# A hybrid encoder trunk: the last convolution products between the first heads' turns and the first scores, and x's operands and first sums reordered

## The chip, the cores and the metric

The kernel runs on one core of one Trainium2 chip. Its engines are TensorE (PE in the profile, with PEld for its weight loads), VectorE (DVE), ScalarE (ACT), GpSimd (POOL) and SyncE (SP), which here only issues DMAs. Each engine takes its instructions from a queue of its own, in order; semaphores tie them together. The metric is the device time of one execution in microseconds; lower is better.

## The reference

Two layers act on x, 512 tokens by 1024 features, in float32. Each layer is

```python
x = x + 0.5 * swiglu(rms_norm(x, ffn1_norm[l]), ffn1_w_gate[l], ffn1_w_up[l], ffn1_w_down[l])
h = rms_norm(x, mix_norm[l])
p = h @ w_in[l]
attn = mla_group(p[..., :o_kv], p[..., o_kv:o_pe], p[..., o_pe:o_cv], ...)
conv = conv_group(p[..., o_cv:], conv_w[l], conv_b[l], conv_ln_g[l], conv_ln_b[l])
x = x + jnp.concatenate([attn, conv], axis=-1) @ w_out[l]
x = x + 0.5 * swiglu(rms_norm(x, ffn2_norm[l]), ffn2_w_gate[l], ffn2_w_up[l], ffn2_w_down[l])
x = rms_norm(x, post_norm[l])
```

`mla_group` makes queries and keys of 8 heads (96 features each) from low-rank latents, normalises them per head, and runs block-causal softmax attention. `conv_group` takes two halves a and g of 512 channels, forms a * sigmoid(g), convolves each channel with 31 taps along the tokens, and applies a layer norm and a silu. The inner width of `swiglu` is 2816.

## The kernel before

**Layout.** x lies transposed in on-chip memory: 8 tiles of 128 features by 512 tokens. Every product of float32 operands is made of three (`mm3`, L142 to L145): each operand is split into a rounded high part and a low rest, and high-high, high-low and low-high are summed in PSUM. One output tile of 128 by 512 over 1024 inputs is thus 8 x 3 = 24 products. Weights come through `load_w` (L126): a DMA on SP's queue into a raw tile (three buffers), a cast to the high part on ScalarE (L130), the low part on VectorE (L136); high and low tiles have four buffers each. For the first four tiles of w_out the low part comes from ScalarE (L133) and a DMA issued by GpSimd (L134).

**Order of the work.** The program is written as a Python trace. When the kernel is built, a scheduler fills each engine's queue by the order of the trace and by a simulated clock: what is traced earlier goes first where it is ready in that simulation. `tc.issue_after(ins)` adds that whatever the block traces on the engine of `ins` stands behind `ins` in that engine's queue. On the chip the queues are fixed. PSUM has 7 banks in one pool (`bank()`) and one more for the convolution on VectorE.

**FFN** (`ffn_body`). The inner width is worked through in four chunks (`CHUNKS`). In the first chunk four outputs are made by plain products (`plain`, `plain_out`): p = 0 with r = 0 and 1, then p = 1 with r = 0 and 1. x is not normalised ahead of them; the norm is a factor R per token, applied in `plain_out`. Calling `norm()` once makes the sums of squares over all features (eight narrow matmuls at L186), and from them 1/sqrt per token (VectorE, GpSimd); the second call spreads it over the partitions (a product at L205) and copies it to R. From R on, a generator `operands(R)` makes the normalised x and its sums and differences, in 31 steps, which the later chunks need for a Strassen-like product (`pair`, seven products instead of eight). `advance(n)` traces n of these steps: 6 after each output of p = 1, and 3 after each of the 8 down products of the first chunk. In the very first FFN the first weights (`w0`) are loaded beside x, and the squares of x are made by ScalarE and summed by VectorE (L179) at the start.

**Mix** (`mix_body`). `SEQ` (L40) gives the order of its steps: query latents (`q0`, `q1`, `q2`), convolution inputs of four channel groups (first one untitled, then `c1`, `c2`, `c3`), latent keys, `uq` (queries), `uk` (keys and values), and last `c2` and `c3`. A convolution input is two groups of 24 products (`conv_in`) and a gate `glu` (L429): VectorE scales the second group by R (L431), ScalarE takes the sigmoid (L433), VectorE scales the first group (L435) and multiplies (L437). Then the attention: for each head `turn` transposes q and k on TensorE into two banks (L616, L621) and has them evacuated by ScalarE (L618) and VectorE (L623); `scores` (L639) makes four blocks of scores in three banks, VectorE takes their maxima (L641) and ScalarE the exponentials (L645); `turn_p` (L660), `values` (L673) and `turn_out` (L691) follow with lags of some steps (`ORDER`), so that the heads overlap. Traced behind the attention, and so filling idle time, is the convolution (L704 to L723): groups 0 and 3 on VectorE (L712), groups 1 and 2 by products on ScalarE (L716) that GpSimd adds up (L720). The sum of the four (L734 to L736) is read by a product on TensorE (L738) for the layer norm's mean, and the output projection ends the mix.

In the queue of TensorE before the change, the first scores stand as follows: both groups of `c3`, the turns of heads 0 and 1, the scores of head 0, the turn of head 2, the scores of head 1, and so on.

Of the kernel before, what the change touches and what calls it, by code (L numbers as in the profile page):

```python
# [11 lines left out]
AF = mybir.ActivationFunctionType  # L12
# [23 lines left out]
RING = 41  # L36
CHUNKS = ((0, 2), (2, 5), (5, 8), (8, 11))
CONV = "DAAD"
PAUSE = 16
SEQ = "q0 R c1 q1 q2 qo k kt tt uq uk c2 c3"  # L40
POOLW = "wo"
QFOLD = 0
GLUP = 0
# [24 lines left out]
def encoder_kernel(ctx: ExitStack, tc: tile.TileContext, xT, consts, vecs, rgain, wgu1, wd1,  # L68
# [22 lines left out]
    def bank():  # L91
        return psum.tile([P, S], FP, tag="ps", name=nm("ps"))
# [148 lines left out]
    def ffn_body(fpool, l, gx, norm, wgu, wd, gain, done, w0):  # L241
# [12 lines left out]

        def plain(os, ws, ks):
            for gu, o in enumerate(os):
                for k in ks:
                    w = ws[k % 2]
                    c = slice(gu * 512 + k // 2 * P, gu * 512 + (k // 2 + 1) * P)
                    mm3(o, w[0][:, c], w[1][:, c], gx[k][0], gx[k][1], k == 0, k == KD - 1)  # L260
# [118 lines left out]
        for p0, p1 in CHUNKS:  # L379
            f0, fn = 2 * p0, 2 * (p1 - p0)  # L380
            act = []
            for p in range(p0, p1):
                if p == 0:
                    os = []
                    for r in range(2):
                        ws = w0 if r == 0 and w0 else [load_w(wgu[l, p, 2 * r + q], WC) for q in range(2)]
                        os.append([bank(), bank()])
                        plain(os[r], ws, range(KD - 1))
                        plain(os[r], ws, range(KD - 1, KD))
                        R = norm()  # L390
                    steps = operands(R)
                    for o in os:
                        act.append(plain_out(o, R))
                elif p < CHUNKS[0][1]:
                    for r in range(2):
                        ws = [load_w(wgu[l, p, 2 * r + q], WC) for q in range(2)]
                        o = [bank(), bank()]
                        plain(o, ws, range(KD))
                        advance(6)
                        act.append(plain_out(o, R))  # L400
                else:
                    act += pair(p)
            for m in range(KD):
                pd = bank()
                group(pd, load_w(wd[l, m, :, f0 * P:(f0 + fn) * P], fn * P), act, range(fn), fn)
                if p0 == 0:
                    advance(3)
                V.scalar_tensor_tensor(x[:, m, :], pd, 0.5, x[:, m, :], ALU.mult, ALU.add)  # L408
                if p1 == NF // 2:
                    done(m)  # L410
            if p0 == 0:
                advance(99)
# [12 lines left out]
    def mix_body(kpool, l, gx, norm, done):  # L425
# [3 lines left out]
        def glu(pa, pg):  # L429
            tg = tmp()  # L430
            V.tensor_tensor(tg, pg, R, ALU.mult)  # L431
            sg = tmp()
            A.activation(sg, tg, AF.Sigmoid)  # L433
            ta = tmp()
            V.tensor_tensor(ta, pa, R, ALU.mult)  # L435
            uc = slot()
            (G if GLUP else V).tensor_tensor(uc, ta, sg, ALU.mult)  # L437
            u.append(uc)
# [174 lines left out]
        def turn(h):  # L613
# [4 lines left out]
            A.activation(qT[0:DQ], ps[0:DQ], AF.Copy, scale=gqs[0:DQ])  # L618
            ps = bank()
            for t in range(NT):  # L620
                T.transpose(ps[0:DQ, t * P:(t + 1) * P], kn[:, t, h], ident)  # L621
            kT = slot()
            V.tensor_scalar(kT[0:DQ], ps[0:DQ], gk, None, ALU.mult)  # L623
            heads[h]["qk"] = qT, kT
# [67 lines left out]
            at.append(split(ps))  # L692

        STAGES = [({"t": turn, "s": scores, "p": turn_p, "v": values, "o": turn_out}[c], int(d)) for c, d in zip(ORDER[::2], ORDER[1::2])]
        for step in range(H + 6):
            for stage, lag in STAGES:
                if 0 <= step - lag < H:
                    stage(step - lag)


        with tc.issue_after(order["keys"]):
# [252 lines left out]
```

## Time and profile before

| what | value |
|---|---|
| time, median of 3 runs | 1857.87 us (1856.27 to 1859.78) |
| the profiled execution, its own time | 1857.87 us |
| its span, first to last instruction | 1856.1 us |
| mean granted clock of TensorE | 0.992 of full speed |
| ScalarE's busy time | 937.3 us (50%) |
| VectorE's busy time | 1354.5 us (73%) |
| GpSimd's busy time | 334.2 us (18%) |

The profile is of one execution. A row of the timeline gives the start in us from the span's beginning, the duration, the engine, the line of the kernel, the operation, the tile written, the tiles read, the sizes, how many alike were merged, and in brackets the idle time of the engine just before, with the instruction that ended it. Durations of neighbouring matmuls overlap, since they are pipelined: their spacing is the difference of the starts. A view of windows gives for each stretch its length, the busy time and count of PE, PEld, DVE, ACT and POOL, the clock granted to TensorE, the DMA engines' share and GB/s. In the view of waits a row is: engine, tile and line that waited, whom for, us in total, times, the longest.

### The profile page before, as it was taken

The page shows a single profiled execution, that of the slowest core. Times are in us where ns is not written, and L with a number is a line of the kernel's source. Part 1 is how long each engine was busy: PE and PEld are TensorE (multiplying, and loading weights), DVE is VectorE, ACT ScalarE, POOL GpSimd, SP SyncE. Part 2 cuts the span into 40 slices and gives each one's busy share as a digit, 9 for nine tenths or more (in the row PEclk, how much of TensorE's full clock was granted, in tenths as well). Part 3 has the DMA queues.
Part 4 walks back from the last instruction along what each step waited for, and adds up shares of the span by engine and source line. Part 5 has one row for each costly group of instructions (what it writes and reads, how often), then busy time and mean ns, then how long its engine had stood idle before and what let it go on. Part 6 is the DMA issues. An engine that isn't in the chain of part 4 may idle for free.

```text
span 1856.1 us, 27852 instructions
## 1 busy us (share of the span) xinstructions
PE 1815.4 (98%) x11248; PEld 1623.2 (87%) x11248; DVE 1354.5 (73%) x1764; ACT 937.3 (50%) x1470; POOL 334.2 (18%) x238
## 2 busy tenths in 40 slices
PE   8999999999999999999999999999999999999997
PEld 6898989888788798989888999998978788989895
DVE  6885767588956985757779676766978659767673
ACT  4453535457943453535635444444778434535352
POOL 1000000248933000000310000002688410000002
PEclk9999999999999999999999999999999999999998
DMA  5142422324123142422512424223250322424221
GB/s 218 52 148 68 137 63 86 114 78 133 35 75 102 29 151 66 139 67 94 169 52 72 140 66 140 66 83 114 72 148 1 118 70 63 143 62 143 63 86 63
DMA packets 55569, 175.72 MB, mean 95 GB/s; under 512 B 6160, under 2 KB 6544, under 8 KB 55440
## 3 DMA queue, kind: packets, MB, share of 16 engines
q1 hardware_dynamic: 53856, 169.37, 29.2%
q0 software_dynamic: 1152, 4.19, 1.3%
q8 instruction: 88, 1.44, 0.3%
q10 hardware_dynamic: 432, 0.38, 0.1%
q14 instruction: 41, 0.34, 0.1%
HBM read 171.82 MB, written 2.10 MB: 94 GB/s over the span
## 4 chain that ended last, share of the span: by engine, by line
PE 81%; DVE 9%; ACT 4%; POOL 3%; issue 2%; DMA 0%; SPq 0%; DVEq 0%; POOLq 0%; ACTq 0%
PE ps L143 25%; PE ps L145 25%; PE ps L144 25%; PE ps L673 2%; PE ps L639 2%; DVE wl L136 2%; ACT pr L716 1%; DVE r L292 1%; POOL y L720 1%; PE ps L660 1%; DVE t L297 1%; DVE cv L712 1%; DVE x L408 1%; ACT wh L130 1%; POOL sck L161 0%
## 5 line engine op out<-in xcount | busy, mean ns | idle before, releaser
L143 PE MATMUL ps<-r,wh 128*128 128x256 f32 (+1 forms) x3280 | 1053.2, 327 | 8.7 <-ACT wh L130 6.8
L145 PE MATMUL ps<-r,wl 128*128 128x256 f32 (+1 forms) x3280 | 1052.5, 325 | 6.9 <-DVE wl L136 3.4
L144 PE MATMUL ps<-r,wh 128*128 128x256 f32 (+1 forms) x3280 | 1059.0, 324 | 0.0
L143 PEld LDWEIGHTS ps<-r,wh 128*128 128x128 f32 x3280 | 620.2, 190 | 64.6 <-ACT wh L130 7.8
L145 PEld LDWEIGHTS ps<-r,wl 128*128 128x128 f32 x3280 | 621.1, 190 | 60.2 <-DVE wl L136 5.7
L144 PEld LDWEIGHTS ps<-r,wh 128*128 128x128 f32 x3280 | 624.4, 190 | 52.3 <-issue 2.4
L232 ACT CAST wh<-fr 128x1024 fp32r<-128x1024 f32 x216 | 226.4, 1050 | 299.9 <-PE ps L144 235.8
L130 ACT CAST wh<-raw 128x768 fp32r<-128x768 f32 (+4 forms) x214 | 187.9, 886 | 336.1 <-PE ps L144 164.5
L234 DVE TENSOR_TENSOR wl<-fr,wh 128x1024 fp32r<-128x1024 f32 x216 | 263.5, 1222 | 73.9 <-ACT wh L232 70.9
L179 POOL TENSOR_TENSOR acc<-acc,t 128x512 f32<-128x512 f32 x46 | 79.1, 1728 | 1309.3 <-ACT t L175 1308.5
L136 DVE TENSOR_TENSOR wl<-raw,wh 128x768 fp32r<-128x768 f32 (+4 forms) x198 | 208.2, 1055 | 129.9 <-ACT wh L130 128.6
L408 DVE SCALAR_TENSOR_TENSOR x<-ps,x 128x512 f32<-128x512 f32 x128 | 87.4, 687 | 120.1 <-PE ps L145 120.1
L720 POOL TENSOR_TENSOR y<-y,pr 128x509 f32<-128x509 f32 (+15 forms) x120 | 157.6, 1315 | 53.3 <-ACT pr L716 45.9
L712 DVE SCALAR_TENSOR_TENSOR cv<-r,vec,cv 128x511 f32<-128x511 f32 (+14 forms) x120 | 87.7, 731 | 3.1 <-ACT cv L708 1.7
L716 ACT ACTIVATE pr<-r,vec 128x511 f32<-128x511 f32 (+14 forms) x120 | 84.1, 726 | 6.9 <-POOL y L720 6.7
L150 DVE TENSOR_TENSOR r<-t,r 128x512 fp32r<-128x512 f32 x96 | 64.7, 686 | 13.0 <-ACT r L149 13.0
L149 ACT CAST r<-t 128x512 fp32r<-128x512 f32 x96 | 55.7, 619 | 31.3 <-DVE t L269 18.5
L232 ACT CAST wh<-raw 128x1024 fp32r<-128x1024 f32 x36 | 37.7, 1048 | 65.5 <-PE ps L144 65.5
L234 DVE TENSOR_TENSOR wl<-raw,wh 128x1024 fp32r<-128x1024 f32 x36 | 44.1, 1224 | 26.7 <-ACT wh L232 26.7
L334 ACT COPY t<-ps 128x512 f32<-128x512 f32 x72 | 41.8, 581 | 30.5 <-PE ps L145 30.5
L345 DVE TENSOR_TENSOR raw<-fr,fr 128x1024 f32<-128x1024 f32 x36 | 44.0, 1223 | 17.6 <-DMA fr<-in_wgu 17.6
L639 PE MATMUL ps<-r,r 96*128 96x384 f32 (+3 forms) x128 | 48.5, 497 | 7.9 <-DVE r L623 3.9
(170 smaller groups left out, 1611.8 us busy)
## 6 DMA issues: line engine op xcount, KB each, us to landing
fr<-in_wgu SPq DMA_DIRECT2D x144, 512.0 KB, 3.6
raw<-in_wd SPq DMA_DIRECT2D x96, 384.0 KB, 3.1
raw<-in_wgu SPq DMA_DIRECT2D x32, 512.0 KB, 3.6
raw<-in_wd SPq DMA_DIRECT2D x32, 256.0 KB, 2.7
raw<-in_wcv SPq DMA_DIRECT2D x16, 512.0 KB, 3.6
raw<-in_wout SPq DMA_DIRECT2D x16, 512.0 KB, 4.2
wl<-in_wout POOLq DMA_DIRECT2D x8, 512.0 KB, 6.7
raw<-in_wql SPq DMA_DIRECT2D x6, 512.0 KB, 3.5
```

Source lines behind the costliest of these rows:

```text
L130: A.copy(hi[:, :w], raw[:, :w])
L136: (G if kind in POOLW.split() else V).tensor_tensor(lo[:, :w], raw[:, :w], hi[:, :w].bitcast(FP), ALU.subtract)
L143: T.matmul(o, lh, rh, start=first, stop=False, skip_group_check=free)
L144: T.matmul(o, lh, rl, start=False, stop=False, skip_group_check=free)
L145: T.matmul(o, ll, rh, start=False, stop=last, skip_group_check=free)
L232: A.copy(hi[:, :w], src[:, :w])
L234: V.tensor_tensor(lo[:, :w], src[:, :w], hi[:, :w].bitcast(FP), ALU.subtract)
L408: V.scalar_tensor_tensor(x[:, m, :], pd, 0.5, x[:, m, :], ALU.mult, ALU.add)
L639: T.matmul(o, qT[0:DQ, i * P:(i + 1) * P], kT[0:DQ, 0:n], start=True, stop=False)
L712: V.scalar_tensor_tensor(acc[:, s:], u[c][:, :S - s], tap(k), acc[:, s:], ALU.mult, ALU.add)
L716: A.activation(pr[:, s:], u[c][:, :S - s], AF.Copy, scale=tap(k))
L720: order["conv"] = G.tensor_tensor(acc[:, s:], acc[:, s:], pr[:, s:], ALU.add).ins
```

## The change

Three things are reordered. Every operation of the kernel stays; none is added.

First, `c3` leaves `SEQ`. Its first group of products is traced where it was, its second group's weights are loaded, then the first two heads (`AHEAD`) are turned, then come the second group, held behind the last transpose of these turns in TensorE's queue, the gate, and the scores of head 0, whose ScalarE work is held behind the gate's sigmoid. The loop over the heads leaves out what has been done.

Second, in the very first FFN the first call of `norm()` moves from the end of r = 0 to the middle of r = 1, between its gate and its up products; the second call comes at the end of r = 1 as before. `plain` takes None for an output that is left out.

Third, `advance` takes 8 steps instead of 6 after each output of p = 1, and 2 instead of 3 after each down product.

```diff
+AHEAD = 2
-SEQ = "q0 R c1 q1 q2 qo k kt tt uq uk c2 c3"
+SEQ = "q0 R c1 q1 q2 qo k kt tt uq uk c2"
...
-                for k in ks:
+                for k in ks if o is not None else ():
...
-                        plain(os[r], ws, range(KD - 1))
-                        plain(os[r], ws, range(KD - 1, KD))
+                        if r and w0:
+                            plain(os[r][:1], ws, range(KD))
+                            norm()
+                            plain([None] + os[r][1:], ws, range(KD))
+                        else:
+                            plain(os[r], ws, range(KD - 1))
+                            plain(os[r], ws, range(KD - 1, KD))
+                            if not w0:
+                                R = norm()
+                    if w0:
                         R = norm()
...
-                        advance(6)
+                        advance(8)
...
-                    advance(3)
+                    advance(2)
...
-            A.activation(sg, tg, AF.Sigmoid)
+            order["gate"] = A.activation(sg, tg, AF.Sigmoid).ins
...
-                T.transpose(ps[0:DQ, t * P:(t + 1) * P], kn[:, t, h], ident)
+                order["turned"] = T.transpose(ps[0:DQ, t * P:(t + 1) * P], kn[:, t, h], ident).ins
...
+        pa, pg = bank(), bank()
+        group(pa, load_w(wcv[l, 6], WC), gx, range(KD), KD)
+        wlast = load_w(wcv[l, 7], WC)
+        for h in range(AHEAD):
+            turn(h)
+        with tc.issue_after(order["turned"]):
+            group(pg, wlast, gx, range(KD), KD)
+        glu(pa, pg)
+        with tc.issue_after(order["gate"]):
+            scores(0)
         for step in range(H + 6):
             for stage, lag in STAGES:
-                if 0 <= step - lag < H:
-                    stage(step - lag)
+                h = step - lag
+                if 0 <= h < H and not (stage is turn and h < AHEAD or stage is scores and h == 0):
+                    stage(h)
```

## The prediction

> **What bounds the kernel now.** I read the page first: how full TensorE is, and which engine the chain that ended last runs through.
>
> ```profile
> span 1856.1 us, 27852 instructions
> ...
> PE 1815.4 (98%) x11248; PEld 1623.2 (87%) x11248; DVE 1354.5 (73%) x1764; ACT 937.3 (50%) x1470; POOL 334.2 (18%) x238
> ...
> PE 81%; DVE 9%; ACT 4%; POOL 3%; issue 2%; DMA 0%; SPq 0%; DVEq 0%; POOLq 0%; ACTq 0%
> ```
>
> TensorE is busy for all but 41 us (1856.1 less 1815.4), and the chain runs through it for 81%. The change adds and removes no product, so all it can win lies in TensorE's idle time and in time at a lower clock. Next, the view of waits for TensorE: whom it waited for, total us, times, longest.
>
> ```profile
> PE ps L639 <- DVE r L623: 3.9, 1, 3.9
> PE ps L639 <- ACT r L618: 3.4, 1, 3.4
> PE ps L145 <- DVE wl L136: 3.4, 7, 1.8
> ...
> PE ps L145 <- DVE wl L234: 3.0, 4, 0.9
> ...
> PE ps L186 <- DVE acc L179: 1.4, 1, 1.4
> ```
>
> The two longest waits that the change touches are one hole per layer: the first scores (L639) wait for the first head's turned q and k, evacuated at L618 and L623. L186 is the first sum of squares, at the start. The L145 waits lie in the first chunk of the four FFNs. The timeline of TensorE, layer 0 (start us, duration, line, tiles, count, idle before):
>
> ```profile
> 456.36 0.39 PE L143 MATMUL ps<-r,wh 128*128 128x512 f32 x1
> ...
> 461.80 0.60 PE L616 MATMUL ps<-cst,q 128*96 128x128 f32 x4
> ...
> 462.67 0.60 PE L616 MATMUL ps<-cst,q 128*96 128x128 f32 x4
> ...
> 467.08 0.80 PE L639 MATMUL ps<-r,r 96*128 96x128 f32 x2 [3.37 <-ACT r L618]
> ...
> 471.15 1.07 PE L616 MATMUL ps<-cst,q 128*96 128x128 f32 x4
> ...
> 472.87 0.46 PE L639 MATMUL ps<-r,r 96*128 96x128 f32 x2
> ...
> 481.91 0.64 PE L621 MATMUL ps<-cst,kn 128*96 128x128 f32 x4 [0.43 <-ACT r L645]
> 482.38 0.39 PE L639 MATMUL ps<-r,r 96*128 96x128 f32 x2
> ...
> 484.37 1.29 PE L660 MATMUL ps<-cst,r 128*128 128x128 f32 x10
> ```
>
> The hole has two prices. The idle is 3.4 us. Then three score products of head 0 take 467.08 to 471.15, 4.07 us, where the like three of a later head take 482.38 to 484.37, 1.99 us; and the next turn takes 471.15 to 472.87, 1.72 us, where one at 461.80 took 0.87 (to 462.67). That is 2.08 + 0.85 = 2.9 us lost. The view of windows says why (us, then busy time of PE, PEld, DVE, ACT, POOL, then PEclk, the granted clock):
>
> ```profile
> 468.00:471.00 3.00, 3.00 (x5) 1.07 (x6) 2.88 (x5) 2.97 (x6) 2.84 (x3) 0.50 0.91 195
> 473.00:476.00 3.00, 3.00 (x18) 1.92 (x17) 2.89 (x7) 3.00 (x9) 2.91 (x3) 1.00 0.00 0
> 1382.00:1385.00 3.00, 2.90 (x7) 1.78 (x8) 2.12 (x5) 2.97 (x6) 2.78 (x3) 0.50 1.00 223
> 1396.00:1399.00 3.00, 1.84 (x12) 1.22 (x11) 3.00 (x7) 3.00 (x8) 2.84 (x3) 1.00 0.01 3
> ```
>
> After the hole the clock is 0.50, 5 us later 1.00. In layer 1:
>
> ```profile
> 1376.32 0.60 PE L616 MATMUL ps<-cst,q 128*96 128x128 f32 x4
> ...
> 1382.10 0.76 PE L639 MATMUL ps<-r,r 96*128 96x128 f32 x2 [3.87 <-DVE r L623]
> ...
> 1386.14 1.07 PE L616 MATMUL ps<-cst,q 128*96 128x128 f32 x4
> ...
> 1387.83 0.39 PE L639 MATMUL ps<-r,r 96*128 96x128 f32 x2
> ```
>
> 3.9 us idle, and (4.04 - 1.99) + (1.69 - 0.87) = 2.9 us lost at the low clock. Both layers: 3.4 + 2.9 + 3.9 + 2.9 = 13.1 us, the most that filling the hole can give.
>
> **The change, part by part.** *The last group of conv channel 3.* Its 24 products run from 456.36 to 461.80, 5.44 us (0.227 each). Now they stand before the turns; afterwards the two turns (4 x 0.435 = 1.74 us) come first, then the 24 products, then the scores. Nothing is added; 5.44 us of work covers an evacuation that kept TensorE idle for 3.4 and 3.9. The order that it needs: the turns come up to 5.44 us earlier, to 456.36, and read kn, whose last writer on VectorE is L590:
>
> ```profile
> 453.26 1.48 DVE L590 TENSOR_TENSOR kn<-ck,scp 128x256 f32<-128x256 f32 x1
> ...
> 1367.42 1.48 DVE L590 TENSOR_TENSOR kn<-ck,scp 128x256 f32<-128x256 f32 x1
> ```
>
> It ends by 454.74, 1.6 us ahead of 456.36, and in layer 1 by 1368.9, 2.0 us ahead of 1370.9 (1376.32 less 5.44), so the turns don't wait; if kn came later, that wait would be paid one for one. The weight load of the group keeps its place on SP:
>
> ```profile
> 432.38 2.47 SPq L128 DMA_DIRECT2D raw<-in_wcv  x2
> 437.46 27.06 SPq L128 DMA_DIRECT2D raw<-in_wout  x7
> ```
>
> It is issued right behind the other half of channel 3, over 20 us ahead of its use and before w_out's loads; no DMA is moved past another. The group holds its weight buffer until about 463.5 instead of 461.8, so the fourth w_out tile is cast some 1.7 us later; the output projection that reads it starts after 525 (below), which hides that. PSUM has seven banks: two for the conv channel and four for two turns leave one, so the scores' later banks hang on the evacuations and the gate.
>
> What is late next is ScalarE. The gate's sigmoid (L433) needs the moved products; the first exponentials (L645) are queued behind it, and behind these the next head's q (L618) and the products L716 that feed GpSimd's convolution. ScalarE's timeline, layer 0 and 1:
>
> ```profile
> 464.66 0.61 ACT L433 ACTIVATE t<-t 128x512 f32<-128x512 f32 x1
> ...
> 468.91 1.28 ACT L645 ACT_TABLE_LOAD   x1
> ...
> 1378.79 0.62 ACT L433 ACTIVATE t<-t 128x512 f32<-128x512 f32 x1
> ...
> 1382.75 1.28 ACT L645 ACT_TABLE_LOAD   x1
> ```
>
> Now the sigmoid starts 2.86 us after the group's last product (464.66 less 461.80); the first exponential can start at 470.2 (468.91 + 1.28). Afterwards the group ends at 456.36 + 1.74 + 5.44 = 463.5. With the same lag the sigmoid runs 466.4 to 467.0 and the first exponential follows the table at 468.3, only 1.9 us sooner. If TensorE then followed ScalarE one for one, 1.9 us is all that layer 0 wins; in layer 1, where the lag is 2.47 (1378.79 less 1376.32), by the same sum (1376.32 + 1.74 + 2.47 + 0.62 + 1.28 = 1382.4 against 1384.0) 1.6 us. If it doesn't, the layers win 6.3 and 6.8. TensorE's first wait on ScalarE after the scores is at 481.91, 11.7 us behind the first exponential, and only 0.43 us long: between them stand products L716, which can be passed by exponentials. So neither bound is the nearer; I take the middle, (1.9 + 6.3)/2 = 4.1 and (1.6 + 6.8)/2 = 4.2, together **8.3 us**, kept between 3.5 and 13.1.
>
> [...] The window 1396 to 1399 above has TensorE idle for 1.16 of 3 us, in several waits, at a clock of 1.00: short waits did not lower it. [...]
>
> *The first sums.* TensorE at the start:
>
> ```profile
> 20.15 0.39 PE L145 MATMUL ps<-r,wl 128*128 128x512 f32 x1
> 21.97 1.05 PE L186 MATMUL ps<-ones,acc 128*128 128x1 f32 x8 [1.43 <-DVE acc L179]
> ...
> 33.88 1.02 PE L205 MATMUL ps<-t,ones 128*128 128x512 f32 x2
> ```
>
> The sums wait 1.4 us for the squares. Afterwards 24 products (5.44 us) stand ahead of them: the sums run at about 20.4 + 5.4 = 25.8, long after 21.97, and lose the wait. The spread (L205) then follows after the other 24 products, at about 32.3. Today its operand has some 11 us between sums and spread, afterwards 5.4; the short chain on VectorE and GpSimd between them fits if it takes under 5. **1.4 us** won, between 0 and 1.6.
>
> *x's operands.* Eight steps instead of six go before each output of the second pair, two instead of three per down product. The number of VectorE operations is the same; four come earlier in each FFN. In three of the four FFNs VectorE has a hole there, as in the first:
>
> ```profile
> 56.46 0.69 DVE L136 TENSOR_TENSOR wl<-raw,wh 128x512 fp32r<-128x512 f32 x1 [2.69 <-ACT wh L130]
> ```
>
> Four operations of 0.6 us fill 2.4 of these 2.69 us, so VectorE is less late in the chunk behind, where TensorE waits 3.0 us in all for L234 and 3.4 for L136 (view of waits). At most those 6.4 go. Without the hole (layer 1's first FFN) the four steps would delay the last output by 2.4, which is the loss that I allow. Those waits also hang on ScalarE's cast just before, so I take the low part: **1.5 us** won, kept between -2.4 and 6.4.
>
> Sum: 8.3 + 1.4 + 1.5 = 11.2 us. The profiled execution took 1857.87 us, 1.8 around its span of 1856.1, and is itself the median of the three runs; 1857.87 - 11.2 = **1846.7 us**.
>
> **The rivals.**
> *TensorE sets the pace (1841.9).* Exponentials pass the products L716, and the whole 13.1 us is won: 1857.87 - 13.1 - 1.4 - 1.5. For it: the one wait of 0.43 us. Against: ScalarE was busy 3.00 of 3 us in 473 to 476.
> *The clock falls anyway (1852.5).* Bank waits behind the first scores add up; the 5.8 us at 0.50 stay: 8.3 - 5.8 + 2.9 = 5.4 us won. For it: seven banks, the gate and the table load between scores and exponentials. Against: the 1396 row.
> *It doesn't do what it says (1856.5).* The queues are ordered when the kernel is built; the hole may merely move behind the scores, where TensorE waits as long for banks. Then only the first sums win, 1.4.
> *Slower (1863.5): the convolution becomes the end of the mix.* GpSimd's chain and the product that reads its sum, layer 0:
>
> ```profile
> 489.24 24.77 POOL L720 TENSOR_TENSOR y<-y,pr 128x500 f32<-128x500 f32 x19 [0.40 <-ACT pr L716]
> ...
> 516.67 1.27 POOL L736 TENSOR_TENSOR t<-t,r 128x512 f32<-128x512 f32 x1
> ...
> 525.62 1.02 PE L738 MATMUL ps<-t,onesm 128*128 128x512 f32 x2
> ```
>
> The sum is ready at 517.94, 7.7 us before TensorE reads it. With TensorE 4.1 us sooner 3.6 are left. If exponentials crowd out the products L716, GpSimd, which adds one per 1.30 us (24.77/19) and was kept full, falls behind; from 3.6 us on, each us of slip costs one. A slip of 12 us, nine adds, in both layers (the second taken like the first) gives about -11.2 + 2 x 8.4 = 5.6 us slower. Against: the exponentials' total is unchanged, and ScalarE only shifts them by about 4 us.
>
> **How the numbers follow.** Forecast 0.55, of its own accord 1843 to 1851; TensorE's pace 0.20; clock 0.12; nothing but the sums 0.07; slower 0.06. About 0.2%, 3.7 us, can be told from no change. Faster by more: 0.55 + 0.20 + 0.12 = 0.87; within: 0.07; slower: 0.06. The range goes down to 1841 (the second case) and up to 1855: the lower bounds 3.5 + 1.4 - 2.4 = 2.5 us won give 1855.4, and the clock rival lies inside.
>
> **What would show it.** Right: the first scores of both layers start within 0.3 us of the group's last product; granted clock 1.00 from 463 to 476; the L186 wait gone; the first exponential 1.5 to 4 us sooner. Wrong: waits of the scores or turns on L645 of over 3 us per layer, a wait of L738 on GpSimd, or longer L145 waits in the FFNs' first chunks.

## The result, and the profile after

| kernel | median | lowest to highest |
|---|---|---|
| before, 6 runs | 1858.09 us | 1856.27 to 1860.00 |
| changed, 6 runs | 1843.52 us | 1842.28 to 1845.00 |

The ratio is 0.9922, with a 95% interval of 0.9909 to 0.9935: 14.6 us less, where 11.2 were forecast. The profiled execution took 1843.94 us. In the changed kernel every line number behind the first edit is one or more higher: `mm3` is L144 to L146, the turns L625 and L630, the scores L648, the exponentials L654.

The page of the changed kernel, first its span and the busy times, then the chain:

```profile
span 1842.1 us, 27874 instructions
...
PE 1809.1 (98%) x11248; PEld 1620.3 (88%) x11248; DVE 1354.1 (74%) x1764; ACT 937.1 (51%) x1470; POOL 336.2 (18%) x238
...
PE 84%; DVE 8%; POOL 3%; ACT 3%; issue 2%; DMA 0%; DVEq 0%; SPq 0%; POOLq 0%; ACTq 0%
```

The count of products is the same, and TensorE's idle time fell from 40.7 to 33.0 us (1842.1 less 1809.1), so 7.7 of the 14.0 us of span were idle time. The other 6.3 us came out of its busy time, which holds the same products: part of it is less time at a low clock (below). The view of waits of TensorE says what became of the waits:

```profile
PE ps L648 <- ACT r L654: 5.4, 2, 3.4
...
PE ps L146 <- DVE wl L137: 1.9, 4, 0.6
...
PE ps L146 <- DVE wl L235: 1.4, 1, 1.4
PE ps L630 <- DVE r L672: 1.2, 2, 0.9
```

The wait of the first sums (L187) is gone, and those of the FFNs' first chunks, 3.4 and 3.0 us before, are 1.9 and 1.4. But the scores still have a wait of 3.4 us. The timeline of TensorE, layer 0, from the group's last product on, shows where it now stands:

```profile
458.91 0.39 PE L146 MATMUL ps<-r,wl 128*128 128x512 f32 x1
459.14 0.38 PE L648 MATMUL ps<-r,r 96*128 96x128 f32 x2
...
466.56 0.70 PE L648 MATMUL ps<-r,r 96*128 96x256 f32 x2 [3.37 <-ACT r L654]
...
467.13 2.00 PE L648 MATMUL ps<-r,r 96*128 96x512 f32 x2
...
468.99 1.07 PE L625 MATMUL ps<-cst,q 128*96 128x128 f32 x4
```

The first scores follow the group's last product by 0.23 us: the hole that the change aims at is closed. TensorE then makes the first head's scores, a turn and two blocks of the second head, and stops for 3.37 us, as long as before, until the first exponential frees a bank. In layer 1 the same stop is shorter:

```profile
1370.91 0.38 PE L648 MATMUL ps<-r,r 96*128 96x128 f32 x2
...
1377.00 0.70 PE L648 MATMUL ps<-r,r 96*128 96x256 f32 x2 [2.04 <-ACT r L654]
...
1378.54 1.06 PE L625 MATMUL ps<-cst,q 128*96 128x128 f32 x4
```

What holds the exponentials back is seen in ScalarE's timeline, layer 0:

```profile
460.45 1.04 ACT L131 CAST wh<-raw 128x1024 fp32r<-128x1024 f32 x1
461.39 0.70 ACT L737 ACTIVATE pr<-r,vec 128x486 f32<-128x486 f32 x1
461.99 1.05 ACT L134 ACTIVATE wl<-raw 128x1024 fp32r<-128x1024 f32 x1
462.94 0.62 ACT L442 ACTIVATE t<-t 128x512 f32<-128x512 f32 x1
463.46 1.28 ACT L737 ACTIVATE pr<-r,vec 128x485 f32<-128x485 f32 x2
464.75 1.28 ACT L654 ACT_TABLE_LOAD   x1
466.05 0.37 ACT L654 ACTIVATE r<-ps,mx 128x128 f32<-128x128 f32 x1
```

The queue has no gap. The cast and the low part of the fourth w_out tile and a convolution product stand ahead of the gate's sigmoid (L442), two more products between it and the table load. TensorE's third block of the second head starts 0.51 us behind the first exponential. The view of windows gives the clock (the column before the DMA share):

```profile
467.00:471.00 4.00, 4.00 (x18) 2.60 (x16) 1.26 (x3) 4.00 (x13) 2.05 (x2) 0.57 0.60 108
471.00:475.00 4.00, 3.96 (x24) 2.55 (x23) 4.00 (x8) 4.00 (x11) 2.84 (x4) 1.00 0.00 0
...
1379.00:1383.00 4.00, 4.00 (x17) 3.08 (x16) 2.95 (x6) 4.00 (x12) 2.08 (x2) 0.63 0.05 9
```

So the clock fell behind both stops. A figure such as 0.57 is the mean of a stretch in which the clock changed. In narrower windows it is 1.00 or 0.50; layer 0, three windows of the changed kernel, then one of the kernel before:

```profile
466.00:467.10 1.10, 0.54 (x3) 0.40 (x4) 0.00 (x0) 1.09 (x6) 1.02 (x2) 1.00 0.97 168
467.20:470.55 3.35, 3.35 (x13) 2.06 (x12) 1.12 (x2) 3.35 (x10) 1.40 (x2) 0.50 0.62 119
470.65:472.00 1.35, 1.31 (x9) 0.92 (x8) 1.14 (x2) 1.35 (x5) 0.96 (x2) 1.00 0.00 0
```

```profile
466.25:472.95 6.70, 5.87 (x18) 3.73 (x19) 6.08 (x10) 6.67 (x14) 6.25 (x6) 0.50 0.72 178
```

In these two profiles the part at the low clock is smaller than before. In layer 0 the 512-wide block takes 1.86 us (467.13 to 468.99) instead of 0.97, and the turn 1.67 (468.99 to 470.66) instead of 0.87: 1.7 us lost, against 2.9. In layer 1 the turn and the two score blocks behind it are the slow ones: 1.6 us lost, against 2.9.

To say where the 14 us came from, I take the start of each row of sums of squares (L186 before, L187 after), which stands at the border of each stage, and subtract. Gains in us, from one profiled execution of each kernel:

| kernel | start and FFN 1, layer 0 | mix 0 | FFN 2, layer 0 | FFN 1, layer 1 | mix 1 | FFN 2, layer 1 | all |
|---|---|---|---|---|---|---|---|
| changed | 4.4 | 1.0 | 2.3 | -0.6 | 4.5 | 2.1 | 13.8 |
| attn_only | -0.1 | 1.7 | 0.3 | -0.5 | 4.2 | 0.0 | 5.6 |
| sums_only | 2.4 | 0.0 | 0.0 | 0.0 | 1.7 | 0.0 | 4.1 |
| opnd_only | 1.9 | -0.4 | 2.4 | -0.6 | 1.4 | 2.1 | 6.7 |
| exp_first | 4.1 | 2.1 | 2.4 | -2.1 | -0.1 | 2.1 | 8.5 |
| cast_late | 4.2 | 1.5 | 2.3 | -1.9 | 2.3 | 2.1 | 10.5 |
| opnd_three | 4.1 | 1.2 | 2.3 | -1.8 | 4.8 | 2.1 | 12.7 |
| swap | 3.8 | 1.6 | 2.4 | -2.1 | 4.9 | 2.0 | 12.6 |
| cast_late_v | 3.6 | -3.2 | 2.3 | -0.6 | -0.1 | 2.0 | 4.1 |
| best | 4.4 | -2.3 | 2.3 | 0.0 | -0.9 | 2.1 | 5.6 |
| swap_late | 4.5 | -1.1 | 2.4 | -2.1 | 3.9 | 2.1 | 9.6 |
| changed, again | 3.7 | 0.4 | 2.4 | -3.2 | 3.1 | 2.1 | 8.4 |

The last row is the unaltered changed kernel in another profiled execution, and the first row's equal but for chance: the first FFN and the mix of layer 1 differ by 2.6 and 1.4 us between the two. The table is read with that in mind.

### The profile page after: what moved, and what is told of

It is laid out like the page before. It is cut to its first block, busy times and chain, and to the rows that moved or that the text cites. A ratio compares the mean times of both kernels' runs of the same rounds, so it can differ in the third digit from the quotient of the medians.

```text
span 1842.1 us, 27874 instructions
## 1 busy us (share of the span) xinstructions
PE 1809.1 (98%) x11248; PEld 1620.3 (88%) x11248; DVE 1354.1 (74%) x1764; ACT 937.1 (51%) x1470; POOL 336.2 (18%) x238
## 3 DMA queue, kind: packets, MB, share of 16 engines
q8 instruction: 88, 1.44, 0.3%
## 4 chain that ended last, share of the span: by engine, by line
PE 84%; DVE 8%; POOL 3%; ACT 3%; issue 2%; DMA 0%; DVEq 0%; SPq 0%; POOLq 0%; ACTq 0%
PE ps L144 26%; PE ps L146 26%; PE ps L145 26%; PE ps L682 2%; PE ps L648 2%; DVE wl L137 1%; POOL y L741 1%; DVE cv L733 1%; DVE r L293 1%; PE ps L669 1%; ACT pr L737 1%; DVE t L298 1%; ACT wh L131 1%; POOL sck L162 0%; PE ps L187 0%
## 5 line engine op out<-in xcount | busy, mean ns | idle before, releaser
L144 PE MATMUL ps<-r,wh 128*128 128x256 f32 (+1 forms) x3280 | 1052.3, 327 | 7.9 <-ACT wh L131 6.9
L146 PE MATMUL ps<-r,wl 128*128 128x256 f32 (+1 forms) x3280 | 1051.8, 324 | 3.9 <-DVE wl L137 1.9
L144 PEld LDWEIGHTS ps<-r,wh 128*128 128x128 f32 x3280 | 619.9, 190 | 63.1 <-ACT wh L131 7.9
L146 PEld LDWEIGHTS ps<-r,wl 128*128 128x128 f32 x3280 | 620.9, 190 | 57.2 <-DVE wl L137 4.9
L741 POOL TENSOR_TENSOR y<-y,pr 128x511 f32<-128x511 f32 (+14 forms) x120 | 157.4, 1312 | 57.8 <-ACT pr L737 50.8
L648 PE MATMUL ps<-r,r 96*128 96x384 f32 (+3 forms) x128 | 46.0, 476 | 5.4 <-ACT r L654 5.4
L157 DVE SCALAR_TENSOR_TENSOR r<-x,vec,r 128x512 fp32r<-128x512 f32 x40 | 45.9, 1158 | 4.3 <-ACT r L156 4.3
```

The costliest lines, as they stand in the source:

```text
L144: T.matmul(o, lh, rh, start=first, stop=False, skip_group_check=free)
L146: T.matmul(o, ll, rh, start=False, stop=last, skip_group_check=free)
L648: T.matmul(o, qT[0:DQ, i * P:(i + 1) * P], kT[0:DQ, 0:n], start=True, stop=False)
L741: order["conv"] = G.tensor_tensor(acc[:, s:], acc[:, s:], pr[:, s:], ALU.add).ins
```

## The experiments

### Each part alone

The first three kernels hold one of the three parts each; the other two parts are as before.

```diff
# attn_only: sums and operands as before
-                        if r and w0:
...
+                        plain(os[r], ws, range(KD - 1))
+                        plain(os[r], ws, range(KD - 1, KD))
+                        R = norm()
...
-                        advance(8)
+                        advance(6)
...
-                    advance(2)
+                    advance(3)
```

> The changed attention order alone (conv group between the turns and the first scores); first sums and operands as before. Theory 1, the parts add up: the stages of the two traces (changed against before) put the two mixes at 1.0 + 4.5 = 5.5 us, so this kernel takes 1858.1 - 5.5 = 1852.6, with a wait of TensorE on the exponentials of head 0 of about 3.4 us in layer 0 and 2 in layer 1. Theory 2, the prediction's size of 8.3 us was right and layer 0's 1.0 is so small only because the other two parts bring TensorE 4.4 us sooner to a stage whose other engines are not sooner: 1858.1 - 8.3 = 1849.8, and the wait in layer 0 is under 2 us with no low clock behind it.

Measured: 1852.69 us (1852.04 to 1854.08) against 1858.98 before on the same chip, ratio 0.9966 (0.9952 to 0.9980): 6.3 us. TensorE waits 3.3 and 2.0 us for an exponential, as in the changed kernel. The hole behind the scores belongs to the attention order alone.

```diff
# sums_only: attention order and operands as before
-SEQ = "q0 R c1 q1 q2 qo k kt tt uq uk c2"
+SEQ = "q0 R c1 q1 q2 qo k kt tt uq uk c2 c3"
...
-                        advance(8)
+                        advance(6)
...
```

> The first sums alone, moved behind the gate half of r = 1; all else as before. Theory 1: the wait of 1.4 us at the sums goes and nothing else moves: 1858.1 - 1.5 = 1856.6; the spread (first one) then stands at about 32.3 us of the span where it stood at 33.9. The 2.4 us that the changed kernel's trace shows up to the spread are 1.6 of the wait and 0.8 from a clock that rose at 9.9 us instead of 12.1, which this kernel may or may not show. Theory 2: all 2.4 us come of the order and come back here: 1855.7.

Measured: 1854.86 us (1852.54 to 1856.21), ratio 0.9977 (0.9966 to 0.9987): 4.1 us, of which 2.4 lie before the first mix. The 1.7 us in the second mix, which this part doesn't touch, show how far the place of single instructions in the fixed queues moves a stage: the kernel before has three waits for exponentials later in that mix (below), this one has none of them.

```diff
# opnd_only: attention order and sums as before, advance(8) and advance(2) kept
-SEQ = "q0 R c1 q1 q2 qo k kt tt uq uk c2"
+SEQ = "q0 R c1 q1 q2 qo k kt tt uq uk c2 c3"
...
-                        if r and w0:
...
+                        R = norm()
...
```

> The operand steps alone, 8 and 2 for 6 and 3; all else as before. Theory 1: what the stages of the traces show comes from these steps: the first FFN 2.0, the second 2.3, the third -0.6 (there VectorE has no hole, and x is rescaled in the same place), the fourth 2.1, together 5.9 us: 1852.2. Theory 2, my forecast of 1.5 us, the rest coming from how TensorE meets ScalarE and VectorE after the other parts: 1856.6. The waits of TensorE at the low parts in the first chunks should fall from 1.8 to about 0.4 us per FFN by theory 1, and stay over 1 by theory 2.

Measured: 1853.99 us (1850.96 to 1855.67), ratio 0.9968 (0.9956 to 0.9981): 5.0 us. Three of the four FFNs gain 1.9 to 2.4 us each. The three parts add up to 6.3 + 4.1 + 5.0 = 15.4 us, against 14.6 together: they hardly touch one another.

### Is layer 1's first FFN the price of the operand steps?

```diff
# opnd_three
-                        advance(8)
+                        advance(6 if norm.after else 8)
...
-                    advance(2)
+                    advance(3 if norm.after else 2)
```

> The changed kernel with the operand steps back at 6 and 3 in the one FFN (layer 1's first) in which x is rescaled. Theory 1: there the four steps cost 0.6 us, since VectorE has no hole for them; the stage gets that back and nothing else moves: 1843.5 - 0.6 = 1842.9. Theory 2: the 0.6 is a matter of where a queue has its sums, not of the steps: 1843.5.

Measured: 1845.36 us (1844.98 to 1847.58), ratio 0.9930 (0.9918 to 0.9943), no better than the changed kernel. With the old steps this FFN lost 1.8 us in the profile. TensorE waited 3.9 us in its first chunk (1.78, 1.45 and two together 0.67), against 2.7 with the new steps. So taking the steps back doesn't mend that stage in this kernel. The steps alone don't make it worse either: the kernel best (below) has the same old steps there, waits of 1.78, 0.33 and 0.28 us much as before the change, and loses nothing in this FFN. What the steps cost there hangs on the order of the other work in the queues.

### Exponentials ahead of their neighbours

Two kernels move what stands ahead of the first exponentials in ScalarE's queue. The first holds back the fourth w_out cast and the convolution products of the second group from the shift by 26 tokens on, and all of the third:

```diff
# exp_first
-            wo = [load_w(wout[l, m], WC, "sum") for m in range(WOP)]
+            wo = [load_w(wout[l, m], WC, "sum") for m in range(WOP - 1)]
+        with tc.issue_after(heads[0]["e3"]), tc.issue_after(order["keys"]):
+            wo.append(load_w(wout[l, WOP - 1], WC, "sum"))
...
-                    A.activation(pr[:, s:], u[c][:, :S - s], AF.Copy, scale=tap(k))
+                    with tc.issue_after(heads[0]["e3"]) if c > 1 or s >= 26 else nullcontext():
+                        A.activation(pr[:, s:], u[c][:, :S - s], AF.Copy, scale=tap(k))
```

(`heads[0]["e3"]` is head 0's last exponential.)

> The changed kernel, with the cast of the fourth w_out tile and the convolution's products on ScalarE from the 26th tap of group 1 on held behind the last exponential of head 0. Theory 1: the hole that the change moved behind the first scores (3.4 us in layer 0, 2.0 in layer 1, and 1.7 us each at the low clock behind it) is ScalarE's queue, in which two to three us of casts and products stand ahead of the sigmoid and 1.2 between it and the table load. Without them the first exponential starts some 3 us sooner, the wait falls under 1 us, the clock stays up: 3.4 + 1.7 + 2.0 + 1.7 - 2 x 1 = 6.8 us less than the changed kernel, 1836.7. Theory 2: GpSimd, starved of products, ends the convolution later and the gain is given back where TensorE reads the sum of the groups: within 2 us of 1843.5. Theory 3: the exponentials need the sigmoid's chain through VectorE and are no sooner: 1843.5.

Measured: 1849.20 us (1848.86 to 1849.55), ratio 0.9946 (0.9933 to 0.9958), the median 5.7 us above the changed kernel's. The timelines of this kernel, ScalarE's first exponential and GpSimd in layer 0, then the product that reads GpSimd's sum in layer 1:

```profile
462.73 0.37 ACT L654 ACTIVATE r<-ps,mx 128x128 f32<-128x128 f32 x1
...
468.22 0.88 POOL L135 DMA_DIRECT2D wl<-in_wout  x1 [4.07 <-ACT wl L134]
...
1432.42 2.07 PE L762 MATMUL ps<-t,onesm 128*128 128x512 f32 x2 [2.31 <-POOL t L760]
```

The exponential came 3.3 us sooner (462.73 against 466.05) and the stop of 3.37 us went; three shorter waits, of 0.53, 1.14 and 0.49 us, came in its place, the clock stayed at 1.00 from 464 to 480, and the first mix gained 2.1 us. But GpSimd stood idle for 4.07 us: its DMA for the fourth tile's low part waited for the work held back on ScalarE, which made no product for GpSimd to add between 460.89 and 467.81 either. Its sum came later; TensorE waited 0.37 us for it in layer 0 and 2.31 in layer 1, with a granted clock of 0.50 behind the longer wait. In the changed kernel this sum, from GpSimd's and TensorE's timelines, has only 2.0 us left:

```profile
516.90 1.27 POOL L757 TENSOR_TENSOR t<-t,r 128x512 f32<-128x512 f32 x1
...
520.19 1.02 PE L759 MATMUL ps<-t,onesm 128*128 128x512 f32 x2
```

It had 7.7 before the change; in layer 1 it has 1.8. This is the mechanism of the rival "slower", with its place and its price: not reached by the change, and reached by the first step beyond it.

The second kernel holds back only the cast and its low part:

```diff
# cast_late
-            wo = [load_w(wout[l, m], WC, "sum") for m in range(WOP)]
+            wo = [load_w(wout[l, m], WC, "sum") for m in range(WOP - 1)]
+        with tc.issue_after(heads[0]["e3"]), tc.issue_after(order["keys"]):
+            wo.append(load_w(wout[l, WOP - 1], WC, "sum"))
```

> The changed kernel with only the cast and the low part of the fourth w_out tile held behind the last exponential of head 0; the convolution's products are free. 1.9 us leave ScalarE's queue ahead of the first exponential, which starts 1.9 to 2.5 us sooner; TensorE's wait on it falls from 3.4 to about 1.2 in layer 0 and from 2.0 to 0 in layer 1, and the low clock behind it goes. Theory 1, GpSimd's sum is now 2.0 and 1.8 us ahead of the product that reads it, and that is all that can be won per layer: 1843.5 - 3.8 = 1839.7, with a wait of that product on GpSimd of 1 to 2 us. Theory 2, GpSimd keeps pace and all of 2.2 + 1.7 + 2.0 + 1.7 = 7.6 us is won: 1835.9.

Measured: 1845.99 us (1845.91 to 1847.17), ratio 0.9933 (0.9921 to 0.9946). GpSimd's sum came in time, the stop of 3.37 us became 1.56, and yet nothing was won. TensorE's timeline, layer 0, and a row of the windows:

```profile
464.98 0.70 PE L648 MATMUL ps<-r,r 96*128 96x256 f32 x2 [1.56 <-ACT r L654]
467.50 0.64 PE L630 MATMUL ps<-cst,kn 128*96 128x128 f32 x4 [0.35 <-ACT r L654]
469.36 0.70 PE L648 MATMUL ps<-r,r 96*128 96x256 f32 x2 [0.77 <-ACT r L654]
470.77 0.88 PE L648 MATMUL ps<-r,r 96*128 96x384 f32 x2 [0.68 <-DVE r L632]
```

```profile
471.23:475.23 4.00, 4.00 (x16) 2.62 (x15) 3.43 (x6) 4.00 (x14) 3.88 (x4) 0.57 1.01 202
```

The one long stop came apart into four, 3.36 us in all, and the clock fell behind them all the same (0.57 is the mean of that window). In layer 1 none was over 0.77 us, and the clock fell to 0.50.

### GpSimd's last adds on VectorE

```diff
# cast_late_v: cast_late, and
-YP = 1
+YP = 0
...
-        G.tensor_tensor(ysum, ys[0], ys[1], ALU.add)
-        G.tensor_tensor(ysum, ysum, ys[2], ALU.add)
+        V.tensor_tensor(ysum, ys[0], ys[1], ALU.add)
+        V.tensor_tensor(ysum, ysum, ys[2], ALU.add)
```

> As cast_late, and the three additions that sum the four convolution groups on VectorE instead of GpSimd (0.7 instead of 1.3 us each). Theory 1, the convolution's end is the limit: it comes 2 us sooner, so 2 us more per layer are won than in cast_late, about 1836. Theory 2, it isn't: as cast_late.

```diff
# best: cast_late_v with the steps of opnd_three
```

> cast_late_v and opnd_three together. Theory 1: their gains add, 0.6 us under cast_late_v, about 1835.4. Theory 2: the planner orders the later queues anew and part of it is lost: within 1 us of cast_late_v.

Measured: cast_late_v 1855.06 us (1852.10 to 1856.98), ratio 0.9978 (0.9969 to 0.9987); best 1852.39 us (1852.28 to 1854.25), ratio 0.9968 (0.9955 to 0.9980). Both are worse than the changed kernel by 9 to 12 us. The adds freed GpSimd, but on VectorE the last of them stands behind the attention's last work. TensorE's timeline of cast_late_v, layer 0:

```profile
522.81 2.05 PE L761 MATMUL ps<-t,onesm 128*128 128x512 f32 x2 [2.09 <-DVE t L759]
```

The wait of 2.1 us comes in both layers; in layer 0 this product also runs at half its speed behind it (2.05 us, against 1.02 in the changed kernel), in layer 1 nearly at full speed (1.10).

### The two halves of the last input exchanged

If the sigmoid's half is summed first, ahead of the turns, ScalarE can take it before the casts.

```diff
# swap
-        group(pa, load_w(wcv[l, 6], WC), gx, range(KD), KD)
-        wlast = load_w(wcv[l, 7], WC)
+        group(pg, load_w(wcv[l, 7], WC), gx, range(KD), KD)
+        wlast = load_w(wcv[l, 6], WC)
...
-            group(pg, wlast, gx, range(KD), KD)
+            group(pa, wlast, gx, range(KD), KD)
```

> The changed kernel with the two halves of the last convolution input exchanged: the half that needs the sigmoid is summed before the turns, the plain half between the turns and the scores. Theory 1: what holds the first exponentials back is the sigmoid's place in ScalarE's queue, which opens only behind the second group's last product. With the sigmoid's group done earlier, the table load of the exponential follows four convolution products instead of standing 4.03 us (layer 0) behind the second group, so the waits of the third and fourth scores on the exponential of 3.37 and 2.04 us go, with the low clock behind them; up to about 9 us, of which GpSimd's sum, which has 2.0 and 1.8 us left before TensorE asks for it, may let through only some 3.8: 1839.7 us, 1833.5 without that bound. Theory 2: the other short waits (0.85 us on the reduction in layer 0) and GpSimd's sum take what is won, as where the fourth cast was put off: 1843 to 1846 us, with the clock down all the same.

The second kernel, swap_late, is swap with the edit of cast_late.

> The exchanged halves, and the fourth output weight's cast and low part put off behind the first head's last exponential. Theory 1: the two together leave no wait on an exponential over 0.5 us in either layer, and the clock stays at 1.00 through the first head: 1836 to 1840 us. Theory 2: the put-off cast lets GpSimd's last products come later and the short waits of some 0.3 to 0.8 us stay, so it is slower than the exchange alone by 1 to 4 us: 1842 to 1847 us.

The third is the changed kernel itself, on the same chip.

> The changed kernel once more, unaltered, on the chip of the two runs beside it. Both theories: 1843.5 us, between 1842.3 and 1845.0; what differs from it by under 1 us is not told apart.

| kernel | median | lowest to highest | ratio (95%) |
|---|---|---|---|
| swap | 1845.07 us | 1844.34 to 1845.69 | 0.9926 (0.9912 to 0.9939) |
| swap_late | 1848.17 us | 1845.60 to 1848.67 | 0.9941 (0.9928 to 0.9953) |
| changed, again | 1844.39 us | 1844.13 to 1849.21 | 0.9928 (0.9915 to 0.9940) |

The exchange wins nothing that can be told apart from none. In layer 0 the sigmoid now ran at 458.13, but five convolution products, an evacuation, the cast and its low part still stood between it and the table load at 464.26. TensorE's timeline of swap, layers 0 and 1:

```profile
466.07 1.22 PE L648 MATMUL ps<-r,r 96*128 96x256 f32 x2 [2.23 <-ACT r L654]
...
1377.36 0.70 PE L648 MATMUL ps<-r,r 96*128 96x256 f32 x2 [0.80 <-ACT r L654]
```

The stops are 2.23 and 0.80 us instead of 3.37 and 2.04. In layer 0 the granted clock still fell, to 0.50 from 467 to 471; in layer 1 it stayed at 1.00 from 1375 to 1387. In swap_late layer 0 got three waits of 1.27, 1.12 and 2.31 us and the low clock at 472, and lost 1.1 us.

The control shows something else: its profiled execution, the longest of its five at 1849.21 us, has the same waits in layer 1's first FFN as the changed kernel's first profile. TensorE's timelines, the changed kernel first, then the control, the last of these waits:

```profile
994.74 0.39 PE L146 MATMUL ps<-r,wl 128*128 128x256 f32 x1 [1.44 <-DVE wl L235]
```

```profile
996.00 0.58 PE L146 MATMUL ps<-r,wl 128*128 128x256 f32 x1 [1.43 <-DVE wl L235]
```

And the windows behind them, in the same order:

```profile
995.00:1000.00 5.00, 5.00 (x43) 5.00 (x43) 3.09 (x3) 1.54 (x2) 0.00 (x0) 1.00 0.67 205
```

```profile
995.00:1000.00 5.00, 4.00 (x18) 4.00 (x19) 4.36 (x4) 0.91 (x1) 0.00 (x0) 0.53 0.49 118
1000.00:1005.00 5.00, 5.00 (x36) 5.00 (x35) 2.80 (x3) 2.40 (x3) 0.00 (x0) 0.79 0.54 198
```

The same three waits of 0.24, 0.45 and 1.44 us within 3.3 us (0.23, 0.44 and 1.43 in the control) once left the clock at 1.00 and once did not, in one and the same program. This stage lost 0.6 us in the one and 3.2 in the other. The profiles of exp_first, cast_late and swap, with these waits too, show 0.72, 0.75 and 0.66 in that window. So the -1.8 to -3.2 in the table's column for layer 1's first FFN says nothing about the edits of those kernels, except in opnd_three, where the clock was 1.00 and the waits longer.

The traces show where the clock's changes lie. The timelines show a first rise of the clock, from 9.80 us in the changed kernel's first to about 12.5 in cast_late_v; ahead of it the products are 0.43 us apart, behind it 0.23. From there on the clock is 1.00 or 0.50 and nothing between in the traces of the kernel before and of the changed one; in the other profiles the windows that lie wholly inside a fall show 0.50. Ahead of the kernel's last 20 us each fall lasts 3.413 or 6.827 us in these two traces, and 3.4 or 6.8 by the windows of the others. Every change in the two lies a whole number of times 3.413 us behind that first rise (the falls 133 and 401 times before, 134 and 401 changed), and the edges of falls that windows show in eight others lie within 0.1 us of such places, which are called borders here. The control's fall, in narrower windows:

```profile
995.30:998.65 3.35, 2.65 (x12) 2.65 (x13) 3.35 (x4) 0.61 (x1) 0.00 (x0) 0.50 0.48 128
998.75:1002.05 3.30, 3.30 (x17) 3.30 (x17) 0.61 (x1) 1.16 (x2) 0.00 (x0) 0.50 0.78 231
1002.15:1005.00 2.85, 2.85 (x25) 2.85 (x25) 2.80 (x3) 1.14 (x2) 0.00 (x0) 1.00 0.28 111
```

One border is at 995.28, in the middle of the control's longest wait (994.57 to 996.00); in the changed kernel's first profile one is at 992.84, with the first two waits ahead of it and the longest behind it. Idle time alone does not decide: between two borders it was 1.39 us in the control, where the clock then fell, and 1.44 in the other profile, where it didn't. In the traces before and changed every stretch between borders at a clock of 1.00 that had 1.87 us or more of idle time was followed by a fall, and ahead of the kernel's last 20 us none with 1.77 or less was; the control's fall, with 1.39, lies below that, and what tips it there stays open. That the clock is set by what lies between two borders was not shown.

## Why the prediction came out as it did

The forecast was 1846.7 us within 1841.0 to 1855.0, and the median is 1843.52. The gain was right within 3.4 us (11.2 against 14.6), but by terms that miss in opposite directions, so part of that is luck. Against the table's first row: attention 8.3 forecast, 1.0 + 4.5 = 5.5 measured; first sums 1.4 against 2.4, with sums_only; operands 1.5 against 4.4 - 2.4 + 2.3 - 0.6 + 2.1 = 5.8. Of the forecast's 11.2 us the attention was to bring three quarters; it brought 40%. These are figures of one profile each: by the changed kernel's second profile the attention brought 0.4 + 3.1 = 3.5 us, and attn_only's median stands 6.3 us below the kernel before.

**The group that covers the turns: right as a mechanism.** The scores start 0.23 us behind the group's last product in both layers. The turns did not wait for kn, though kn was ready only 0.6 us ahead of the turns in layer 0 (at 451.30; they start at 451.91 with q and read kn at 452.34) and not 1.6: measured from the mix's start, kn came 1.0 us later than before.

**What is late next: named rightly, sized too well.** The prediction said ScalarE's exponentials, through the gate and the banks. The step that failed is "With the same lag the sigmoid runs 466.4 to 467.0 and the first exponential follows the table at 468.3". The lag from the group's end to the sigmoid grew from 2.86 to 3.80 us (459.14 to 462.94). Cast, low part and a product stand right ahead of it in both kernels; ScalarE's timeline before:

```profile
462.17 1.03 ACT L130 CAST wh<-raw 128x1024 fp32r<-128x1024 f32 x1
463.11 1.05 ACT L133 ACTIVATE wl<-raw 128x1024 fp32r<-128x1024 f32 x1
464.07 0.69 ACT L716 ACTIVATE pr<-r,vec 128x487 f32<-128x487 f32 x1
```

What is new stands ahead of these. From the sigmoid before this one on, ScalarE's queue has no gap in either kernel, and between the two sigmoids the changed kernel also has the first two heads' q (L627, 1.1 us) and one more product (0.6). So the cast began 1.31 us behind the group's end (460.45) and not 0.37 (462.17). And the table load did not follow the sigmoid: two convolution products were left between them, so from sigmoid to exponential it was 3.11 us, not 1.9. Together 2.15 us: measured from the mix's start, the first exponential of layer 0 came 0.3 us later than before and not 1.9 sooner (in the span it came 4.15 sooner, which is the earlier start of the mix). TensorE did its scores earlier and waited the same 3.37 us behind them. That is over the 3 us on exponentials that the prediction named as a sign of being wrong; layer 1's 2.04 is not.

So in layer 0 the rival "it doesn't do what it says", whose hole moves behind the scores, described the waits: 0.8 of the 1.0 us is a shorter time at the low clock (1.7 us lost instead of 2.9), less a longer later wait of 0.85 instead of 0.43. In layer 1 the first stop fell by 1.83 us (3.87 to 2.04), the low clock by 1.3, and later waits by 1.05. The last are these of the kernel before, from TensorE's timeline, for which only one of 0.40 us stands after:

```profile
1395.82 0.64 PE L616 MATMUL ps<-cst,q 128*96 128x128 f32 x4 [0.29 <-ACT r L645]
1396.98 0.64 PE L621 MATMUL ps<-cst,kn 128*96 128x128 f32 x4 [0.53 <-ACT r L645]
1398.25 0.49 PE L639 MATMUL ps<-r,r 96*128 96x128 f32 x2 [0.63 <-ACT r L645]
```

That is 4.2 of the 4.5 us measured. The prediction used just these three waits to say that short waits don't lower the clock.

The shorter time at the low clock is not shown to come from the change: in the changed kernel's second profile, with stops of 3.35 and 2.04 us, the clock was low for 6.83 us in each layer, as in the kernel before, and opnd_only, with the old order, had 6.83 us in layer 0 and 3.41 in layer 1.

**The clock: the argument against the rival failed.** The forecast was a clock of 1.00 from 463 to 476; it was 0.50 from 467.18 to 470.60. One window in which short waits left the clock alone was taken for a rule. In cast_late the waits of 0.77 and 0.68 us, together between two borders (468.40 to 471.81), were followed by the low clock, and the one of 1.56, alone between two earlier borders, was not. In exp_first three of 0.49 to 1.14 us didn't lower it, and layer 1's first FFN shows the same waits with both outcomes. The rival "the clock falls anyway" was thus half of what happened: the clock fell in both layers, for a shorter time in the changed kernel's first profile and for as long as before in its second.

**The first sums: right, and a little small.** Their wait of 1.4 us is gone; they start at 25.07 and the spread at 31.47, which is 2.41 us before the 33.88 of the kernel before. About 1.6 us is the stop itself (1.43 idle and about 0.2 beyond it): in the changed kernel's second profile, where full clock came at 12.2 us as before the change, the spread started at 32.21, a gain of 1.67. The rest goes with the start of full clock, which comes at 9.9 us in the changed kernel and 10.1 in sums_only, against 12.1 before, by the spacing of the products. Where the sums stay in their old place such an earlier rise is swallowed by their wait: attn_only had full clock at 11.8 and opnd_only at 11.4, and their sums start at 22.1, behind waits of 1.66 and 1.93 us, where before they started at 21.97 behind 1.43. This part is partly chance, then: the changed kernel's two profiles gain 4.4 and 3.7 us up to the first mix.

**The operands: the low part was the wrong choice.** The step "I take the low part" put 1.5 us on waits of 6.4. The hole of 2.69 us on VectorE did fill, as said. Its timeline in the changed kernel, the same weight part:

```profile
54.05 0.69 DVE L137 TENSOR_TENSOR wl<-raw,wh 128x512 fp32r<-128x512 f32 x1 [0.72 <-ACT wh L131]
```

VectorE is then ahead when the first chunk ends, and the waits for L136 and L234 fall from 6.4 to 3.3 us, those on ScalarE's cast (L232) from 1.3 to 0.7. This is 3.7 of the 5.8 us. The other 2 are about what a stop costs beyond its idle time; the clock there is 1.00 in both. TensorE's timeline before, second FFN of layer 0:

```profile
630.36 0.39 PE L144 MATMUL ps<-r,wh 128*128 128x512 f32 x1
630.97 0.50 PE L145 MATMUL ps<-r,wl 128*128 128x512 f32 x1 [0.23 <-DVE wl L136]
631.30 0.39 PE L143 MATMUL ps<-r,wh 128*128 128x512 f32 x1
```

These starts are 0.61 and 0.33 us apart, against 0.23 without a stop: 0.48 us for an idle time of 0.23, so 0.25 on top. Three of the FFNs have one such stop in the first chunk instead of four and gained 0.7 to 0.8 us beyond their idle time; layer 1's first has four instead of three and lost 0.3 beyond it. Of the loss of 2.4 us that was feared there 0.6 came. What the old steps would cost in that FFN is open: 1.8 us in opnd_three, nothing in best.

**GpSimd: right, with less room than forecast.** Forecast was a slack that falls from 7.7 to 3.6 us; it fell to 2.0, since TensorE came 5.4 us sooner and not 4.1, and nothing waited.

No kernel tried is better than the changed one. What is left in the mix is ScalarE, which is full from 452 to 480 with casts, convolution products and exponentials: in the kernels tried, letting one kind go first shortened TensorE's stop, but other waits or GpSimd's later sum took the gain back. Whether less work for ScalarE in this stretch would win the two stops wasn't tried.

## What to carry to other kernels

A stop that is filled by moving work in front of it comes back behind it when the engine that released it is itself full (here 3.37 us again in layer 0, and 2.04 of 3.87 in layer 1): before counting the stop as won, write out, instruction by instruction, what stands ahead of the next release in that engine's queue. An operation that is moved by a few microseconds on one engine doesn't move its neighbours in another engine's queue with it (the sigmoid's lag grew from 2.86 to 3.80 us), so a lag read from the trace of before can't be carried over. A profile of one execution decides nothing of a microsecond or two where TensorE's short waits lie (two profiles of one kernel differ by 2.6 and 1.4 us in two stages here): take the unaltered kernel's second profile as the measure, and look at the clock in narrow windows, since a mean such as 0.57 hides how long it was low.

## What was not expected of the hardware

- A stop of 2.04 us in layer 1 was followed by the low clock, but only 1.5 us after work had gone on (the score blocks at 1377.00 and 1377.57 still ran at full speed, the turn at 1378.54 at half): the fall stood at 1378.54, 401 times 3.413 us behind the first rise at 9.80, not at the stop. In layer 0 of cast_late no stop was over 1.56 us, and the clock fell.
- One program with the same 2.1 us of short waits at the same place kept the clock at 1.00 in one execution and had 0.50 for 6.83 us in another, which is 2.6 us of difference in that stage.
